# One ring of three PSUM banks for the scores and transposes of two attentions

## The chip, the cores and the metric

The kernel runs on one core of one Trainium2 chip. The metric is the device time of one execution in microseconds (us); a change is judged by the medians of repeated executions. Four engines matter here: TensorE (PE in the profile; PEld is its loading of stationary operands), VectorE (DVE), ScalarE (ACT), and the DMA queues that SyncE (SP), ScalarE and GpSimd (POOL) issue. Each engine works through its own queue of instructions in order and waits at an instruction until the semaphores that it names are there.

## The reference

One encoder block on 512 tokens of width 2048, in float32, batch 1. Cut to what matters here:

```python
h = rms_norm(x, norm1_w) * (1 + sc1) + sh1
qa, ka, va, qb, kb, vb, ga, gb = split(h @ w_in)          # 2048 -> 8704 columns
qa, ka = rope(rms_norm(qa, q_norm_w)), rope(rms_norm(ka, k_norm_w))
ya = softmax(qa @ ka.T / sqrt(128)) @ va                  # 8 heads, 2 key/value heads, all 512 keys
yb = softmax(qb @ kb.T / sqrt(128) + bias) @ vb           # 8 heads, a window of 8x16 keys per query
merged = sigmoid(ga) * (ya @ w_oa) + sigmoid(gb) * (yb @ w_ob)
x = x + g1 * (merged @ w_out)
x = x + g2 * swiglu(rms_norm(x, norm2_w) * (1 + sc2) + sh2)
out = rms_norm(x, final_w)
```

## The kernel before

**Products.** Every float32 operand of a matrix product is held as two tiles in the faster matmul format, a high part and the rest ("h" and "l" in the names: `h0h`, `h0l`). `split` (lines 165 to 170) makes them from a float32 source: ACT copies the high part (L168), DVE subtracts it from the source (L170). `mm3` (lines 184 to 190) then issues three matmuls, L188, L189 and L190, into one bank of PSUM. Weights come by DMA as `raw` tiles and are split into `whl` tiles on the way.

**Banks.** `bank(tag)` hands out the eight banks of PSUM: four named `mm`, two `S`, one `T`, one `Y`. Buffers of one name are handed out in turn, in the order in which the program asks for them, and the next holder of a bank waits until the last reader of the holder before is done.

**The stages around the change**, in the order of the program:

1. The projections of the first query heads, keys and part of the gates, up to about 299 us. `h0` to `h15` are the normalised activations, 128 features each.
2. Attention A, heads 0 to 3 (`att_a`, line 897). A head is four blocks of 128 queries. A block: the scores of 128 queries against 512 keys go into a bank `S` (L188 to L190, `S<-kh,qh`); `softmax` takes the maximum (DVE L862, negated at L863), the exponential with its sum (ACT L866), the reciprocal (DVE L869) and the scaled row (DVE L870, tile `e`); four transposes on PE (L886) put it into the bank `T`; `split` reads that bank into the tiles `pth` and `ptl`. The weighted sums of the values go into the bank `Y` (`Y<-pth,st`), 12 products of 256 columns for each two blocks, and `keep_y` stores them.
3. `gates(sg_a, GA, 12, 16)` (line 901): two passes over all of `h` for four column blocks of the first gate, in `mm` banks, each ending in two sigmoids (ACT L641, tile `go`). Then attention A, heads 4 to 7 (line 903), and the release of its memory, pool `p_a` (line 905).
4. `gates(sg_b, GB, 0, 4)` (line 954): two more such passes. While they run, the list `FORMS` (line 952) makes what the next stage needs, on DVE and ACT: `whole_features` adds high part and rest of `h` back into float32 (L928, tiles `hc` and `hw`), `feature_forms` makes sums and differences of their quarters (L938 to L941, tiles `sa` and `sb`) and splits them (`s05h`, `s07l` and so on, for the groups s = 0 to 3). These tiles lie in the pool `p_o` (line 924), in the memory that `p_a` leaves; a tile there waits for the last use of what it covers.
5. `gates7` and `values7` (lines 990 to 993): projections in a form with seven instead of eight block products (`group7`), by sums of weight blocks that `wforms` makes on DVE (tiles `ta`, `tb`, L696 to L699) and splits. For each group s the products go in the order `ORDER` = 1, 2, 3, 5, 6, 7, 4; product 3 needs `s07`, product 5 needs `s05` and the split of `ta`.
6. Attention B (`att_b`, line 1004), two heads at a time between the projections of the next two heads (lines 1085 to 1103). A half head: scores into a bank `S`, the bias added on the way out (DVE L1021), maximum, exponentials, scaling, four transposes into `T` (L1035), `split`, weighted sums in `Y`.
7. The output projections, the second norm, the SwiGLU and the last norm, from about 860 us.

**What sets the order.** The program is written stage after stage, but the framework lays out each engine's queue when it builds the program: an instruction may go ahead of others that were written earlier where the framework reckons these to be waiting for an operand or a bank. So products of the gate passes, which need nothing from the attentions, stand between the steps of the attentions on PE. This order is fixed before the run; on the chip an engine only waits.

Of the kernel before, what the change touches and what calls it, by code (L numbers as in the profile page):

```python
# [23 lines left out]
T = 512  # L24
# [88 lines left out]
def encoder_block(ctx: ExitStack, tc, xp, xT, c, ada1_w, ada2_w, b_ada, norm1_w, w_in, q_norm_w, k_norm_w, bias,  # L113
                  w_oa, w_ob, w_out, norm2_w, w_gate, w_up, w_down, final_w, rope, out):
    nc = tc.nc
    V, S, G = nc.vector, nc.scalar, nc.gpsimd
# [35 lines left out]
    def bank(tag):  # L152
        return ps.tile([P, 512], F32, tag=tag, name=tag, bufs={"mm": 4, "S": 2, "T": 1, "Y": 1}[tag])
# [12 lines left out]
    def split(hi, lo, src, eng=V, pin=lambda ins: ins):  # L166
        with tc.issue_after(hold[0].ins) if hold else contextlib.nullcontext():
            high = pin(S.activation(hi, src, AF.Copy))  # L168
        with tc.issue_after(hold[1].ins) if hold else contextlib.nullcontext():
            latest[:] = [high, pin(eng.tensor_sub(lo, src, hi))]  # L170

    def pair(pool, tag, width, bufs):
        return (pool.tile([P, width], F32R, tag=tag + "h", name=tag + "h", bufs=bufs),
                pool.tile([P, width], F32R, tag=tag + "l", name=tag + "l", bufs=bufs))
# [10 lines left out]
    def mm3(o, lh, ll, rh, rl, start, stop, n=0, **kw):  # L185
        if n:
            o, rh, rl = in_turn(o, n), streams(rh, n), streams(rl, n)
        nc.tensor.matmul(o, lh, rh, start=start, stop=False, **kw)  # L188
        nc.tensor.matmul(o, lh, rl, start=False, stop=False, **kw)  # L189
        nc.tensor.matmul(o, ll, rh, start=False, stop=stop, **kw)  # L190
# [24 lines left out]
    def slot():  # L215
        pace["due"] = min(pace["due"] + pace["rate"], 1.5)
        if mod["then"] and not fetched and mod["next"] == mod["end"]:
            mod.update(mod["then"].pop())
        if pace["due"] >= 1 and (fetched or mod["next"] < mod["end"]):
            pace["due"] -= 1  # L220
            advance(mods)
# [140 lines left out]
    def fetch():  # L362
        while len(fetched) < mod["loads"] and mod["next"] < mod["end"]:
            n = mod["next"] + {2: 32, 3: 32, 4: -32, 5: -32}.get(mod["next"] // KT, 0)
            w = mod["mw"].tile([P, 1024], F32, tag="mw", name="mw", bufs=mod["loads"])
            mod["queue"].dma_start(w, ada2_w[n * P:(n + 1) * P, :])  # L366
            fetched.append(w)
            mod["next"] += 1
# [485 lines left out]
    def keep_y(h, yb):  # L854
        o = aside.tile([P, T], F32, tag="y", name="yo")
        S.activation(o.rearrange("p (h e i) -> p h e i", e=2, i=P), apart(yb), AF.Copy)
        nc.scalar.dma_start(y_d[h], o)

    def softmax(pool, src, scale, w, bufs=2):

        mx = small.tile([P, 1], F32, tag="mx", name="mx")
        V.reduce_max(mx, src, axis=AX.X)  # L862
        V.tensor_scalar(mx, mx, -scale, None, op0=ALU.mult)  # L863
        e = pool.tile([P, 512], F32, tag="e", name="e", bufs=bufs)[:, :w]
        sm = small.tile([P, 1], F32, tag="sm", name="sm")
        S.activation(e.rearrange("p (e i) -> p e i", e=2), src.rearrange("p (i e) -> p e i", e=2), AF.Exp, bias=mx, scale=scale,  # L866
                     accum_out=sm)
        rs = small.tile([P, 1], F32, tag="rs", name="rs")
        V.reciprocal(rs, sm)  # L869
        V.tensor_scalar(e, e, rs, None, op0=ALU.mult)  # L870
        return e

    def att_a(h, q, j, kv):
        kh, kl = (t[:, kv * T:(kv + 1) * T] for t in kT)
        vs = slice(kv * HD, (kv + 1) * HD)
        pts = []
        for i in range(NT):
            if i % 2 == 0:
                pts.append(pair(p_a, "pt", 2 * T, 3))
            sl = slice(j * T + i * P, j * T + (i + 1) * P)  # L880
            sc = bank("S")
            mm3(sc, q[0][:, sl], q[1][:, sl], kh, kl, True, True, T)
            e = softmax(p_a, sc, SCALE, T)
            tp = bank("T")
            for k in range(NT):
                nc.tensor.transpose(tp[:, k * P:(k + 1) * P], e[:, k * P:(k + 1) * P], ident)  # L886
            hi, lo = (t.rearrange("p (k q) -> p k q", k=NT)[:, :, i % 2 * P:(i % 2 + 1) * P] for t in pts[-1])
            split(hi, lo, tp.rearrange("p (k q) -> p k q", k=NT))
        yb = bank("Y")
        for n, pt in enumerate(pts):  # L890
            ys = yb[:, n * 256:(n + 1) * 256]
            for k in range(NT):
                ks = slice(k * 256, (k + 1) * 256)
                mm3(ys, vA[k][0][:, vs], vA[k][1][:, vs], pt[0][:, ks], pt[1][:, ks], k == 0, k == NT - 1, 256)
        keep_y(h, yb)

    for h in range(4):
        att_a(h, q, h, 0)
# [4 lines left out]
    for h in range(4):  # L903
        att_a(4 + h, q, h, 1)
# [95 lines left out]
    mod.update(mw=p_w, sums=[(p_w, 1), (p_w0, 1)], end=48, loads=3)  # L1000
    fetch()
    p_b = tc.alloc_tile_pool(name="p_b", bufs=1, side="right")

    def att_b(h, q, k, v, vs):

        bm = p_b.tile([P, 512], F32, tag="bm", name="bm", bufs=2)
        nc.scalar.dma_start(bm, bias[h * P:(h + 1) * P, :])
        edge = bm.rearrange("p (g n) -> p g n", g=2)
        inner = edge[:, 1:2].to_broadcast([P, 2, 256])
        by = lambda t: t.rearrange("p (k n) -> p k n", n=P)  # L1010
        rows_of = lambda t, g: t[:, g * P:(g + 1) * P]
        keys_of = lambda t, g: by(t)[:, g - 1:g + 1] if g else by(t)[:, 0::3]
        pt = pair(p_b, "pt", 1024, 2)
        for gs, b2, o in (((1, 2), inner, 512), ((0, 3), edge, 0)):
            sc = bank("S")
            for n, g in enumerate(gs):
                mm3(sc[:, n * 256:(n + 1) * 256].rearrange("p (i e) -> p i e", e=2), *(rows_of(t, g) for t in q),
                    *(keys_of(t, g).rearrange("p e i -> p i e") for t in k), True, True)
            s = p_b.tile([P, 512], F32, tag="sb", name="sb", bufs=2)
            s2v = s.rearrange("p (g n) -> p g n", g=2)  # L1020
            V.scalar_tensor_tensor(s2v, sc.rearrange("p (g n) -> p g n", g=2), SCALE, b2, op0=ALU.mult, op1=ALU.add)  # L1021
            mx, sm, rs = (small.tile([P, 2], F32, tag=t, name=t) for t in ("mx2", "sm2", "rs2"))
            V.reduce_max(mx, s2v, axis=AX.X)
            V.tensor_scalar(mx, mx, -1.0, None, op0=ALU.mult)
            e = p_b.tile([P, 512], F32, tag="e", name="e", bufs=3)
            for n in range(2):
                S.activation(e[:, n * 256:(n + 1) * 256].rearrange("p (e i) -> p e i", e=2),
                             s[:, n * 256:(n + 1) * 256].rearrange("p (i e) -> p e i", e=2), AF.Exp, bias=mx[:, n:n + 1],
                             accum_out=sm[:, n:n + 1])
            V.reciprocal(rs, sm)  # L1030
            for n in range(2):
                V.tensor_scalar(e[:, n * 256:(n + 1) * 256], e[:, n * 256:(n + 1) * 256], rs[:, n:n + 1], None, op0=ALU.mult)
            tp = bank("T")
            for j, at in enumerate((0, 1, 2, 3) if o else (2, 3, 1, 0)):
                nc.tensor.transpose(tp[:, j * P:(j + 1) * P], e[:, at * P:(at + 1) * P], ident)  # L1035
            split(*(t[:, o:o + 512] for t in pt), tp)
            slot()
        yb = bank("Y")
        for n, (kk, at, to) in enumerate(((1, slice(5, 7), slice(2, 4)), (0, slice(3, 5), slice(1, 3)),
                                          (2, slice(0, 8, 7), slice(0, 4, 3)), (3, slice(1, 3), slice(0, 2)))):  # L1040
            mm3(by(yb)[:, to], v[kk][0][:, vs], v[kk][1][:, vs], *(by(t)[:, at] for t in pt), n == 0, n == NT - 1,
                skip_group_check=True)
        o = aside.tile([P, T], F32, tag="y", name="yo")
        for to, src in ((o[:, :320], yb[:, 192:]), (o[:, 320:], yb[:, :192])):
            S.activation(to, src, AF.Copy)
        nc.scalar.dma_start(y_d[8 + h], o)
# [628 lines left out]
```

## Time and profile before

| | us |
|---|---|
| median of 3 runs | 2465.59 (2464.08 to 2469.82) |
| the profiled execution, its own time | 2474.1 |
| its span, first to last instruction | 2472.3 |
| PE busy in the span | 2435.4 |
| DVE busy | 2007.5 |
| ACT busy | 1069.9 |

The profiled execution took 8.5 us (0.34%) more than the median, and 1.8 us of it lie outside its span. Sums below are made against its rows; the difference that they give is then put on the median. Two things help to read it. A matmul's end is modelled, and matmuls overlap: a product of 512 columns is shown 0.38 us long, and the next one starts 0.22 us after it, so PE can lose some tenths of a microsecond between two products and still be shown busy. And every view gives times from the start of the span, so a stage is read by its stretch.

### The profile page before, as it was taken

The page shows a single profiled execution, that of the slowest core. Times are in us where ns is not written, and L with a number is a line of the kernel's source. Part 1 is how long each engine was busy: PE and PEld are TensorE (multiplying, and loading weights), DVE is VectorE, ACT ScalarE, POOL GpSimd, SP SyncE. Part 2 cuts the span into 40 slices and gives each one's busy share as a digit, 9 for nine tenths or more (in the row PEclk, how much of TensorE's full clock was granted, in tenths as well). Part 3 has the DMA queues.
Part 4 walks back from the last instruction along what each step waited for, and adds up shares of the span by engine and source line. Part 5 has one row for each costly group of instructions (what it writes and reads, how often), then busy time and mean ns, then how long its engine had stood idle before and what let it go on. Part 6 is the DMA issues. An engine that isn't in the chain of part 4 may idle for free.

```text
span 2472.3 us, 42367 instructions
## 1 busy us (share of the span) xinstructions
PE 2435.4 (99%) x17327; PEld 2280.1 (92%) x17327; DVE 2007.5 (81%) x2704; ACT 1069.9 (43%) x1466; POOL 150.9 (6%) x255
## 2 busy tenths in 40 slices
PE   7999999999999999999999999999999999999998
PEld 6888888999888888888999999999999998999997
DVE  7995778999677678667899989889989885687877
ACT  5223455544344523237744444444444454433333
POOL 0100000000011111111000000000000010000010
PEclk9999999999999999999999999999999999999999
DMA  9874322455766687867444444445454466546563
GB/s 357 285 253 144 104 89 80 142 185 181 252 211 231 204 302 248 296 215 228 137 154 155 145 162 147 135 147 163 129 171 147 128 196 214 188 155 233 189 250 121
DMA packets 213730, 461.77 MB, mean 187 GB/s; under 512 B 15152, under 2 KB 59552, under 8 KB 204832
## 3 DMA queue, kind: packets, MB, share of 16 engines
q1 hardware_dynamic: 174160, 309.76, 38.4%
q0 software_dynamic: 29872, 132.73, 15.8%
q10 hardware_dynamic: 9504, 16.58, 1.9%
q8 instruction: 136, 2.23, 0.4%
q14 instruction: 58, 0.48, 0.1%
HBM read 412.84 MB, written 46.17 MB: 186 GB/s over the span
## 4 chain that ended last, share of the span: by engine, by line
PE 72%; DVE 14%; issue 6%; DMA 4%; ACT 1%; POOL 0%; DVEq 0%; POOLq 0%; ACTq 0%
PE mm L190 15%; PE mm L189 15%; PE mm L188 15%; PE S L188 6%; PE S L189 6%; PE S L190 6%; DVE whl L170 4%; PE Y L188 3%; PE Y L189 2%; PE Y L190 2%; DVE raw L524 2%; DMA raw<-in_w_down 2%; DMA raw<-in_w_up 1%; PE T L886 1%; DVE g_acc L631 1%
## 5 line engine op out<-in xcount | busy, mean ns | idle before, releaser
L168 ACT ACTIVATE whl<-raw 128x1024 fp32r<-128x1024 f32 (+1 forms) x483 | 453.9, 943 | 671.1 <-PE mm L190 288.4
L170 DVE TENSOR_TENSOR whl<-raw,whl 128x1024 fp32r<-128x1024 f32 (+1 forms) x483 | 517.9, 1087 | 126.3 <-ACT whl L168 125.9
L168 ACT ACTIVATE whl<-ta 128x1024 fp32r<-128x1024 f32 x124 | 131.4, 1059 | 181.8 <-PE mm L190 107.6
L168 ACT ACTIVATE whl<-tb 128x1024 fp32r<-128x1024 f32 x124 | 131.4, 1060 | 174.5 <-PE S L190 109.8
L170 DVE TENSOR_TENSOR whl<-ta,whl 128x1024 fp32r<-128x1024 f32 x124 | 151.2, 1220 | 40.7 <-ACT whl L168 40.1
L388 DVE SCALAR_TENSOR_TENSOR acc<-mw,cact,acc 128x1024 f32<-128x1024 f32 x124 | 158.8, 1281 | 18.3 <-DMA mw<-in_ada_w 17.9
L170 DVE TENSOR_TENSOR whl<-tb,whl 128x1024 fp32r<-128x1024 f32 x124 | 150.9, 1217 | 4.6 <-ACT whl L168 4.5
L366 POOL DMA_DIRECT2D mw<-in_ada_w x113 | 60.3, 534 | 1361.5 <-DVE acc L388 946.5
L697 DVE TENSOR_TENSOR ta<-raw,ta 128x512 f32<-128x512 f32 x124 | 85.2, 687 | 69.3 <-DMA raw<-in_w_down 29.7
L696 DVE TENSOR_TENSOR ta<-raw 128x512 f32<-128x512 f32 x124 | 85.3, 688 | 36.7 <-DMA raw<-in_w_down 34.3
L188 PE MATMUL mm<-x56h,whl 128*128 128x256 f32 x336 | 92.5, 275 | 0.4 <-DVE c L784 0.4
L189 PE MATMUL mm<-x56l,whl 128*128 128x256 f32 x336 | 92.4, 275 | 0.0
L190 PE MATMUL mm<-x56h,whl 128*128 128x256 f32 x336 | 92.4, 275 | 0.0
L189 PE MATMUL mm<-whl,s 128*128 128x256 f32 x320 | 88.2, 276 | 1.0 <-DVE whl L170 0.8
L188 PE MATMUL mm<-x3h,whl 128*128 128x256 f32 x320 | 88.1, 275 | 0.0
L188 PE MATMUL mm<-whl,s 128*128 128x256 f32 x320 | 88.1, 275 | 0.0
L189 PE MATMUL mm<-x3l,whl 128*128 128x256 f32 x320 | 88.0, 275 | 0.0
L190 PE MATMUL mm<-x3h,whl 128*128 128x256 f32 x320 | 88.0, 275 | 0.0
L188 PE MATMUL S<-x56h,whl 128*128 128x256 f32 x320 | 88.0, 275 | 0.0
L189 PE MATMUL S<-x56l,whl 128*128 128x256 f32 x320 | 88.0, 275 | 0.0
L190 PE MATMUL S<-x56h,whl 128*128 128x256 f32 x320 | 88.0, 275 | 0.0
L190 PE MATMUL mm<-whl,s 128*128 128x256 f32 x320 | 88.0, 275 | 0.0
(1879 smaller groups left out, 8910.9 us busy)
## 6 DMA issues: line engine op xcount, KB each, us to landing
raw<-in_w_in SPq DMA_DIRECT2D x133, 512.0 KB, 4.6
mw<-in_ada_w POOLq DMA_DIRECT2D x113, 512.0 KB, 4.5
raw<-in_w_gate SPq DMA_DIRECT2D x92, 512.0 KB, 4.6
raw<-in_w_up SPq DMA_DIRECT2D x88, 512.0 KB, 4.6
raw<-in_w_down SPq DMA_DIRECT2D x88, 512.0 KB, 5.4
raw<-in_ada_w POOLq DMA_DIRECT2D x29, 1024.0 KB, 6.6
raw<-in_w_out SPq DMA_DIRECT2D x48, 512.0 KB, 5.5
ffd<-c SPq DMA_DIRECT2D x10, 1024.0 KB, 4.8
```

The lines of the kernel that those rows point to most:

```text
L168: high = pin(S.activation(hi, src, AF.Copy))
L170: latest[:] = [high, pin(eng.tensor_sub(lo, src, hi))]
L188: nc.tensor.matmul(o, lh, rh, start=start, stop=False, **kw)
L189: nc.tensor.matmul(o, lh, rl, start=False, stop=False, **kw)
L190: nc.tensor.matmul(o, ll, rh, start=False, stop=stop, **kw)
L366: mod["queue"].dma_start(w, ada2_w[n * P:(n + 1) * P, :])
L388: behind(V.scalar_tensor_tensor(acc, part, cact[:, k:k + 1], acc, op0=ALU.mult, op1=ALU.add))
L524: V.scalar_tensor_tensor(raw, raw, 1.0, call, op0=ALU.mult, op1=ALU.mult, accum_out=y)
L631: V.tensor_add(acc, acc, b)
L696: V.tensor_sub(t1, b12, b11)
L697: V.tensor_sub(t2_, b22, t1)
L886: nc.tensor.transpose(tp[:, k * P:(k + 1) * P], e[:, k * P:(k + 1) * P], ident)
```

## The change

The scores and the transposes of both attentions ask for their banks by `bank(next(turns))`, where `turns` goes round S, S, T, in place of `bank("S")` for all scores and `bank("T")` for all transposes. Since two asks for `S` take the two `S` banks in turn, this is one ring of three banks, in the order in which the program asks: scores of block 0, transposes of block 0, scores of block 1, transposes of block 1, and so on.

```diff
+    turns = itertools.cycle("SST")
+
     def att_a(h, q, j, kv):
...
-            sc = bank("S")
+            sc = bank(next(turns))
             mm3(sc, q[0][:, sl], q[1][:, sl], kh, kl, True, True, T)
             e = softmax(p_a, sc, SCALE, T)
-            tp = bank("T")
+            tp = bank(next(turns))
...
     p_b = tc.alloc_tile_pool(name="p_b", bufs=1, side="right")
+    turns = itertools.cycle("SST")
...
-            sc = bank("S")
+            sc = bank(next(turns))
...
-            tp = bank("T")
+            tp = bank(next(turns))
```

No operation is added or taken away by hand, and no other bank, tile or loop is touched. Scores of block i + 2 now take the bank that the transposes of block i had, so they wait until these are split; before, they took the bank of the scores of block i, and waited for its exponential alone. Transposes of a block wait for the exponential of the block before, and no longer for the split of that block's transposes.

The diff does not show what the framework makes of it. The queues of PE, DVE and ACT are laid out anew from the first block of attention A to `gates7`, and again through attention B. Three places follow. The lines of the changed file are two higher in this part (`L928` is `L930`, `L886` is `L888`).

On PE, the end of attention A: the last weighted sums of head 7 (`Y_3685`), and what stands behind them. `mm_3715` and `mm_3716` are the first pass of `gates(sg_b)`, `mm_3852` and `mm_3853` the second and last one; `mm_4041` is the first product of `gates7`. Before:

```order
L188 MATMUL Y_3685<-pth_3643,st_2434 128x256
L189 MATMUL Y_3685<-ptl_3644,st_2434 128x256
L190 MATMUL Y_3685<-pth_3643,st_2434 128x256
L188 MATMUL mm_3716<-h12h_1507,whl_3814 128x512
L189 MATMUL mm_3716<-h12l_1508,whl_3814 128x512
L190 MATMUL mm_3716<-h12h_1507,whl_3814 128x512
```

And with the change:

```order
L190 MATMUL Y_3685<-pth_3643,st_2434 128x256
L190 MATMUL mm_3853<-h14h_1698,whl_3976 128x512
L188 MATMUL mm_3852<-h15h_1713,whl_3976 128x512
L189 MATMUL mm_3852<-h15l_1714,whl_3976 128x512
L190 MATMUL mm_3852<-h15h_1713,whl_3976 128x512
L188 MATMUL mm_3853<-h15h_1713,whl_3976 128x512
L189 MATMUL mm_3853<-h15l_1714,whl_3976 128x512
L190 MATMUL mm_3853<-h15h_1713,whl_3976 128x512
L188 MATMUL mm_4041<-h0h_372,whl_4058 128x256
```

Before, 117 products of 512 columns stand between the last weighted sum and the first product of `gates7`: the end of the first pass, from `h12`, and the whole second pass. With the change 7 are left; the other 110 stand further ahead, between the blocks of heads 0 to 7.

On DVE, in the forms: the splits of the first and second group. Before:

```order
L170 TENSOR_TENSOR s05l<-sa,s05h 128x1024
L170 TENSOR_TENSOR s07l<-sb,s07h 128x1024
L928 TENSOR_TENSOR hc<-h11h,h11l 128x512
L170 TENSOR_TENSOR whl<-raw,whl 128x1024
L938 TENSOR_TENSOR sa<-hw 128x512
L940 TENSOR_TENSOR sb<-hw 128x512
L939 TENSOR_TENSOR sa<-sa,hw 128x512
L170 TENSOR_TENSOR whl<-raw,whl 128x1024
L941 TENSOR_TENSOR sb<-hw,sa 128x512
L170 TENSOR_TENSOR s15l<-sa,s15h 128x1024
L170 TENSOR_TENSOR whl<-raw,whl 128x512
L170 TENSOR_TENSOR s17l<-sb,s17h 128x1024
```

And with the change:

```order
L170 TENSOR_TENSOR s05l<-sa,s05h 128x1024
L170 TENSOR_TENSOR s07l<-sb,s07h 128x1024
L930 TENSOR_TENSOR hc<-h9h,h9l 128x512
L930 TENSOR_TENSOR hc<-h10h,h10l 128x512
L930 TENSOR_TENSOR hc<-h11h,h11l 128x512
L940 TENSOR_TENSOR sa<-hw 128x512
L942 TENSOR_TENSOR sb<-hw 128x512
L941 TENSOR_TENSOR sa<-sa,hw 128x512
L943 TENSOR_TENSOR sb<-hw,sa 128x512
L170 TENSOR_TENSOR s15l<-sa,s15h 128x1024
L170 TENSOR_TENSOR s17l<-sb,s17h 128x1024
```

The splits of gate weights (`whl`) that stood between the forms are gone from here, four in all between the first `hc` and the split of the first `ta`; they stand ahead of the end of attention A now. In both queues all forms stand behind the last split of attention A.

On ACT, the sigmoids of the first gate pass (`go`). Before, they stand behind the last block of head 3:

```order
L856 ACTIVATE yo<-Y 128x512
L168 ACTIVATE qh<-T 128x4x128
L857 DMA y_2440<-yo 128x512
L641 ACT_TABLE_LOAD
L641 ACTIVATE go<-mm 128x512
L168 ACTIVATE qh<-T 128x4x128
```

With the change the first one stands in head 1:

```order
L866 ACTIVATE e,sm<-T,mx 128x512
L641 ACT_TABLE_LOAD
L641 ACTIVATE go<-mm 128x512
L168 ACTIVATE pth<-S 128x4x128
L866 ACT_TABLE_LOAD
L866 ACTIVATE e,sm<-S,mx 128x512
L642 DMA sga_264<-go 128x512
```

A sigmoid between two exponentials brings a table load ahead of it and one behind it. The whole ACT queue has 13 table loads before and 19 with the change; the six more stand in attention A.

## Prediction

> **What bounds the kernel now.** I read the page first, then a table of stretches, then the waits in the two attentions, then the chain that ended last, and then single instructions where that chain leaves PE. The page's span, busy times and shares of the chain:
>
> ```profile
> span 2472.3 us, 42367 instructions
> ...
> PE 2435.4 (99%) x17327; PEld 2280.1 (92%) x17327; DVE 2007.5 (81%) x2704; ACT 1069.9 (43%) x1466; POOL 150.9 (6%) x255
> ...
> PE 72%; DVE 14%; issue 6%; DMA 4%; ACT 1%; POOL 0%; DVEq 0%; POOLq 0%; ACTq 0%
> ```
>
> PE is the bound nearly everywhere, with little to win: 2472.3 less 2435.4 is 37 us for the whole program. The table of stretches (busy time with count for each engine, then granted clock, DMA share, GB/s) has attention A, the rest of the gate passes, the beginning of `gates7`, attention B, and a stretch that I need for the clock:
>
> ```profile
> core 0: us, PE busy (x) PEld busy (x) DVE busy (x) ACT busy (x) POOL busy (x), PEclk, DMA share, GB/s
> 290.00:416.30 126.30, 125.16 (x715) 103.52 (x714) 93.29 (x220) 76.45 (x170) 0.53 (x1) 1.00 0.23 76
> 416.30:441.60 25.30, 25.30 (x120) 22.16 (x119) 25.20 (x35) 13.26 (x15) 0.00 (x0) 1.00 0.34 106
> 441.60:447.10 5.50, 4.43 (x40) 4.24 (x38) 5.50 (x9) 3.60 (x6) 0.00 (x0) 1.00 0.55 148
> 660.00:860.00 200.00, 198.60 (x1017) 168.68 (x1016) 144.50 (x222) 94.00 (x184) 25.26 (x44) 1.00 0.66 218
> 50.00:53.40 3.40, 3.40 (x9) 2.65 (x9) 3.40 (x5) 0.47 (x1) 0.53 (x1) 0.50 0.79 259
> ```
>
> In attention A PE stands idle 126.30 − 125.16 = 1.1 us, in attention B 1.4 us. The stretch 416.3 to 441.6, behind attention A, is the odd one: DVE is busy 25.20 of 25.30 us there, and all of the next 5.5, in which PE idles 1.07. The chain of waits says the same: at 416.57 it goes over to DVE and walks along the forms.
>
> ```profile
> 416.57 2.44 DVE hc L928 x4
> ...
> 441.10 1.13 DVE s27l L170
> ```
>
> So from the end of attention A to the first groups of `gates7` DVE sets the end, and PE only fits because it has the gate passes to do meanwhile. PE's rows at both ends of that stretch (start, length, idle time before):
>
> ```profile
> 416.19 0.28 PE L190 MATMUL Y<-pth,st 128*128 128x256 f32 x1
> 416.31 0.38 PE L188 MATMUL mm<-h12h,whl 128*128 128x512 f32 x1
> ...
> 441.56 0.27 PE L188 MATMUL mm<-h0h,whl 128*128 128x256 f32 x1
> ...
> 445.69 0.28 PE L189 MATMUL mm<-s05l,whl 128*128 128x256 f32 x1
> 447.04 0.38 PE L190 MATMUL mm<-s05h,whl 128*128 128x256 f32 x1 [1.07 <-DVE whl L170]
> ```
>
> The last weighted sum starts at 416.19. 117 gate products run from 416.31 to 441.56, 0.216 us each. The 38 products of `gates7` that can run before the split of `ta` take 441.56 to about 445.80. Then PE waits for that split until 447.04: the cover was 1.2 us too short.
>
> **The tail of attention A.** The change moves 110 of the 117 products ahead of that last weighted sum; 7 remain. The forms can't follow them forward. On DVE they stand behind the last split of attention A, and the first one starts only when the weighted sum that began at 416.19 (0.28 long) is through. DVE's rows, from the first form on, and the row of ACT that the split of `s15` waits for:
>
> ```profile
> 416.51 0.69 DVE L928 TENSOR_TENSOR hc<-h0h,h0l 128x512 f32<-128x512 f32 x1
> ...
> 428.66 1.22 DVE L170 TENSOR_TENSOR whl<-raw,whl 128x1024 fp32r<-128x1024 f32 x1
> 429.80 0.68 DVE L938 TENSOR_TENSOR sa<-hw 128x512 f32<-128x512 f32 x1
> ...
> 431.00 0.68 DVE L939 TENSOR_TENSOR sa<-sa,hw 128x512 f32<-128x512 f32 x1
> 431.61 1.22 DVE L170 TENSOR_TENSOR whl<-raw,whl 128x1024 fp32r<-128x1024 f32 x1
> 432.74 0.68 DVE L941 TENSOR_TENSOR sb<-hw,sa 128x512 f32<-128x512 f32 x1
> ...
> 434.48 0.68 DVE L170 TENSOR_TENSOR whl<-raw,whl 128x512 fp32r<-128x512 f32 x1
> 435.08 1.21 DVE L170 TENSOR_TENSOR s17l<-sb,s17h 128x1024 fp32r<-128x1024 f32 x1
> ...
> 438.75 1.22 DVE L170 TENSOR_TENSOR whl<-raw,whl 128x1024 fp32r<-128x1024 f32 x1
> 439.88 1.22 DVE L170 TENSOR_TENSOR s25l<-sa,s25h 128x1024 fp32r<-128x1024 f32 x1
> ```
> ```profile
> 431.72 1.06 ACT L168 ACTIVATE s15h<-sa 128x1024 fp32r<-128x1024 f32 x1 [4.44 <-DVE sa L939]
> ```
>
> From the first form (416.51) to the product that waits for the `ta` split (447.04) DVE takes 30.53 us. Four splits of gate weights leave this stretch; from start to next start they take 1.14 + 1.13 + 0.60 + 1.13 = 4.0 us. One wait comes in: with the `whl` split gone, `s15l` follows `sb` at once, 1.2 us after the start of `sa` at 431.00, while ACT's half of it ends at 432.78, 1.8 us after: 0.6 us. So DVE needs 30.53 − 4.0 + 0.6 = 27.1 us, and it starts 0.32 us after the last weighted sum (416.51 − 416.19).
>
> PE has 7 × 0.216 = 1.5 us of gate products and the 4.24 us of `gates7` (445.80 − 441.56), from 0.12 us after that sum. It is ready for the `ta` split at 5.9 us and gets it at 27.4 us. The wait is 21.5 us where it was 1.2: **+20.3 us.** The same from the other side: the attention ends 110 × 0.216 = 23.7 us later, and DVE's chain behind it is 3.4 shorter. The wait falls into two: some 5 us at the first `s07` product (ACT's `s07h` is ready about 9 us after the sum, PE 4.3 after it) and about 15 at `s05`. The removed splits cost nothing where they now stand: DVE is idle 126.30 − 93.29 = 33 us in attention A and gains 23.7 us of room there.
>
> **The clock after the gap.** One more row of PE, ahead of the stretch at 50.0 that the table shows at clock 0.50:
>
> ```profile
> 49.08 0.48 PE L600 MATMUL mm<-whl,h2h 128*128 128x512 f32 x1 [3.35 <-ACT whl L168]
> ```
>
> After 3.35 us without work PE ran 3.4 us at half its clock, which loses 1.7 us. Gaps of 5 and 15 us should bring this at least once where PE has work: **+1.7 us**, bounds 0 (it falls into the wait) and 3.4 (twice).
>
> **Attention A itself.** The waits in 290 to 416.3, first of PE, then of its loading of stationary operands, which a running product covers in part:
>
> ```profile
> PE S L188 <- ACT e L866: 0.4, 1, 0.4
> ```
> ```profile
> PEld T L886 <- DVE ptl L170: 5.1, 17, 0.4
> PEld S L188 <- ACT e L866: 2.6, 8, 0.8
> ```
>
> The wait of transposes for the split of those before (17 times) is what a second bank takes away; visible on PE is only 0.4 us of all this. I count −1, and at most −8 (5.1 + 2.6). Against it stands the chain from scores to transposes of one block:
>
> ```profile
> 374.65 0.38 PE L190 MATMUL S<-kh,ql 128*128 128x512 f32 x1
> 375.07 0.69 DVE L862 TENSOR_REDUCE mx<-S 128x1 f32<-128x512 f32 x1 [0.55 <-PE S L190]
> ...
> 376.31 0.69 ACT L866 ACTIVATE e<-S,mx 128x512 f32<-128x512 f32 x1 [0.21 <-DVE mx L863]
> ...
> 377.53 0.48 DVE L870 TENSOR_SCALAR e<-e,rs 128x512 f32<-128x512 f32 x1
> ```
>
> Without other work between: 0.42 to the maximum, 0.69 for it, some 0.2 for the negation, 1.22 from exponential to scaling, 0.48: 3.0 us. Where the scores lie in `T`, the new order of PE often puts 11 weighted sums (0.11 each) and 6 gate products between them and their transposes, 2.7 us with the last score product itself. About ten of 32 blocks are so tight: 10 × 0.3 = +3 us. Then the table loads:
>
> ```profile
> 371.58 1.28 ACT L866 ACT_TABLE_LOAD   x1 [0.18 <-DVE mx L863]
> 372.88 0.69 ACT L866 ACTIVATE e<-S,mx 128x512 f32<-128x512 f32 x1
> ```
>
> Six more at 1.28 us are 7.7 us of ACT, which is busy 76 of 126 us here. They come at three places where two or more microseconds of gate products stand on PE anyway; I count +0.5 at each, +1.5 in all, and 7.7 at most. The Trainium skill's page "ScalarE: Activation LUTs", section "What ACT_TABLE_LOAD costs", has a drain of about 1.38 us beside the load at every switch; by it the most would be 16 us, and the sum about 2 us higher. The trace shows no such drain: the exponential starts at 372.88, right behind the load, so the row decides.
>
> Attention A: −1 + 3 + 1.5 = **+3.5 us**. Bounds: −8, and 32 × 0.3 + 7.7 = +17.
>
> **Attention B.** Its order has gate or projection products enough on every side, and its end isn't followed by work that hangs on it: the next products are of `w_oa`. PE's waits there for the attention come to this row:
>
> ```profile
> PE T L1035 <- ACT e L1027: 0.8, 2, 0.4
> ```
>
> I take **0**, between −1 (its 0.8 gone) and +5 (16 half heads at 0.3). The rest of the program keeps its order.
>
> Sum: 20.3 + 1.7 + 3.5 + 0 = +25.5 us on the profiled 2474.1. That execution lies 8.5 us over the median; the difference goes on the median: 2465.6 + 25.5 = **2491.1 us**, 1% slower.
>
> **The rivals.** First, the ring pays in the attentions. The Trainium skill's page "Perfetto Trace Analysis", section "Optimizing Tensor Performance", says that independent groups of matmuls should rotate through different banks, so that the evacuation of one overlaps the next. It speaks for this change. As a mechanism here: the 7.7 us of waits above and 0.8 in attention B go, and the tight blocks don't show. Then 20.3 + 1.7 − 8.5 = +13.5 us, 2479 us. For it: 17 of 32 transposes do wait for a split. Against it: PE's own row shows hardly any of that. 5%.
>
> Second, it costs more in the attentions: every block waits and the table loads stand on the path, to the upper bounds of A and B. 20.3 + 3.4 + 17 + 5 = +46 us, 2511 us; I take all above +37 for this. For it: the chain of a block is now in one line with the split of the one two before. Against it: there are 23.7 us more of gate products in the stretch. 9%.
>
> Third, not slower: the forms aren't held by the last weighted sum. If the pool's tiles lay only over tiles that are read early, and DVE came to the forms under the last heads, the stretch of 27.1 us would be covered again, as before. The point from which it decides is a first `hc` 20 us or more ahead of the last `Y` product; then −1 to −8 of the attentions stay, 2458 to 2465 us. Against it: the row of 416.51 starts as that product ends (416.19 + 0.28), and the queue has all forms behind the last split. 3%, two of which would show as faster.
>
> Last, that nothing moves: the rows of the order under the change say otherwise. 1%, 2465.6 us.
>
> **The numbers.** The forecast (+15.4 to +36.4: the tail at 20 to 21.5, the clock 0 to 3.4, the attentions from −5 to +12, not all ends at once) has 82%, more than that 9%, less but still slower 5%, no change or faster 4%. The range 2481 to 2502 us leaves out about 18%. A measurement of this kernel can tell about 0.2%, 5 us, from no change: faster 2%, the same 2%, slower 96%.
>
> **What would show it.** Right: a first `hc` just behind the last `Y` product of head 7; DVE unbroken from there for 27 us; PE idle about 5 us at the first `s07` product and about 15 at the first L190 of `s05`, released by `whl` L170; then a stretch of clock 0.50; attention A later in ending by about 24 us, with PE's idle time in it by a few microseconds over 1.1; attention B as before. Wrong: PE idle under 10 us between attention A and the second group of `gates7`, or a difference that sits in the attentions or behind 860 us.

## The result and the profile after

The changed kernel takes 2499.24 us (median of 4 runs, 2497.56 to 2502.53) against 2466.61 us before (4 runs, 2464.08 to 2469.82): 1.0133 times as long, 95% interval 1.0116 to 1.0151, or 32.6 us more. The profiled execution took 2499.32 us, 25 us more than the profiled one before. The page, in the three lines that the prediction showed of before:

```profile
span 2497.5 us, 42404 instructions
...
PE 2440.6 (98%) x17327; PEld 2281.6 (91%) x17327; DVE 2015.6 (81%) x2704; ACT 1081.0 (43%) x1472; POOL 151.0 (6%) x255
...
PE 70%; DVE 15%; issue 7%; DMA 3%; ACT 2%; POOL 0%; DVEq 0%; ACTq 0%; POOLq 0%
```

PE's busy time has grown by 5 us, the span by 25: PE waits. The table of stretches (start and end, length, busy time and count of PE, PEld, DVE, ACT and POOL, granted clock, DMA share, GB/s) says where. Its rows are attention A, two parts of the gap behind it, the first products after the gap, and attention B:

```profile
288.00:440.70 152.70, 149.02 (x813) 120.92 (x812) 101.74 (x222) 88.32 (x176) 0.53 (x1) 1.00 0.23 73
440.70:450.00 9.30, 4.66 (x34) 4.13 (x32) 9.06 (x14) 4.97 (x6) 0.00 (x0) 1.00 0.50 172
450.00:468.20 18.20, 4.09 (x18) 3.64 (x17) 17.70 (x25) 6.45 (x8) 0.00 (x0) 0.50 0.09 27
468.20:474.00 5.80, 5.80 (x43) 5.80 (x43) 5.80 (x9) 2.10 (x3) 0.00 (x0) 0.80 0.35 99
694.00:874.30 180.30, 177.07 (x913) 149.86 (x913) 131.63 (x205) 81.61 (x162) 23.02 (x40) 1.00 0.61 197
```

Attention A holds 110 instructions of PE more and is 29 us longer; in the 27.5 us behind it PE has 8.75 us of work, and DVE hardly a pause. PE's waits between 440.7 and 475 us (what it waited for: us in total, times, longest):

```profile
PE mm L188 <- ACT whl L168: 12.8, 1, 12.8
PE mm L188 <- ACT s07h L168: 4.6, 1, 4.6
PE mm L189 <- DVE s07l L170: 1.3, 1, 1.3
```

The chain of waits walks along the forms, as the prediction drew it, and ends at the product that waited 12.8 us:

```profile
440.72 0.13 PE Y L190
440.87 2.49 DVE hc L930 x4
443.36 2.41 DVE hw L930 x4
...
462.78 1.14 DVE s27l L170
...
465.76 1.06 ACT whl L168
466.87 0.58 PE mm L188
```

For the comparison of all kernels I use one more figure: the time between the starts of consecutive PE instructions of a stretch, less what the same instructions take when packed (0.2155 us for 512 columns, 0.1115 for 256, 0.109 for 128, the medians of neighbours in these traces). What is left is time that PE lost there. "Attention A" runs from its first score to its last weighted sum, "the tail" from there to about the first L190 of `s05`, the product that waits for the split of `ta`, and "groups behind" over the products with forms that follow. Us lost, and in the first column the length of attention A and the time of one row of it (128 queries of one head, 32 rows; the mean of the 31 steps from scores to scores):

```
kernel                         A, a row     to A's norm  A     tail   groups behind  B     the rest
before                         123.5, 3.69   21.5         8.3   1.4    0.8           8.0    13.9
before, a second execution     123.6, 3.69   17.6         8.3   1.4    0.8           7.9    11.2
after                          152.5, 4.67   16.9        13.6  21.4    1.4          10.7    15.4
ring in A alone                152.5, 4.67   17.3        13.6  21.4    2.3           8.0     7.3
ring in B alone                123.5, 3.69   18.9         8.3   1.4    0.8          10.7    10.8
ring, gate pass held back      151.4, 4.65   17.5        31.7   3.6    1.9          10.7    11.2
ring, later forms later        152.5, 4.67   18.1        13.5   6.4   14.8          10.9    11.7
skewed ring in A               123.8, 3.77   16.3         8.6   1.4    0.8           8.0     8.6
ring, no scaling in A          139.5, 4.21   16.9         9.7  13.3    1.2          10.7    10.7
before, no scaling in A        123.0, 3.67   19.8         7.8   1.4    0.8           8.1     6.5
skewed ring in B               123.5, 3.69   17.2         8.3   1.4    0.8           9.4     8.2
skewed ring in both            123.8, 3.77   17.1         8.6   1.4    0.8           9.4     6.1
ring, no sigmoid in gates      144.1, 4.43   18.1        12.1  15.4    1.2          10.7    12.0
```

So the change costs 5.3 us in attention A, 20.0 in its tail, 0.6 in the groups behind and 2.7 in attention B: 28.6 us. The two outer columns differ by up to 5 and 9 us among kernels that are alike there; the profiled execution before had the largest loss of all at the start, and so the two profiled executions stand 25 us apart, the medians 32.6. In two kernels, those with the gate pass held back and without the sigmoid, some 1.4 us more are lost where no column counts, between the norm and attention A; the clock stands at half there for 3.4 us.

The mean of a row hides one long step: between heads 3 and 4 stand most products of the first gate (`sg_a`), 34.2 us in the kernel before and 18.6 us in the changed one, which has more of them between the rows ahead. The other 30 steps take 2.67 us each before and 4.21 after.

### The profile page after: what moved, and what is told of

Same layout as the page of the kernel before. It is cut to its first block, busy times and chain, and to the rows that moved or that the text cites. A ratio compares the mean times of both kernels' runs of the same rounds, so it can differ in the third digit from the quotient of the medians.

```text
span 2497.5 us, 42404 instructions
## 1 busy us (share of the span) xinstructions
PE 2440.6 (98%) x17327; PEld 2281.6 (91%) x17327; DVE 2015.6 (81%) x2704; ACT 1081.0 (43%) x1472; POOL 151.0 (6%) x255
## 4 chain that ended last, share of the span: by engine, by line
PE 70%; DVE 15%; issue 7%; DMA 3%; ACT 2%; POOL 0%; DVEq 0%; ACTq 0%; POOLq 0%
PE mm L190 14%; PE mm L188 14%; PE mm L189 14%; PE S L189 5%; PE S L190 5%; PE S L188 5%; DVE whl L170 3%; PE Y L188 2%; PE Y L189 2%; PE Y L190 2%; DVE raw L524 2%; DMA raw<-in_w_down 2%; DMA raw<-in_w_up 1%; PE T L188 1%; PE T L190 1%
## 5 line engine op out<-in xcount | busy, mean ns | idle before, releaser
L168 ACT ACTIVATE whl<-raw 128x1024 fp32r<-128x1024 f32 (+1 forms) x483 | 454.1, 943 | 664.1 <-PE mm L190 281.0
L188 PE MATMUL mm<-x56h,whl 128*128 128x256 f32 x336 | 92.6, 276 | 0.4 <-DVE c L784 0.4
L190 PE MATMUL mm<-x56h,whl 128*128 128x256 f32 x336 | 92.4, 275 | 0.0
L188 PE MATMUL mm<-x3h,whl 128*128 128x256 f32 x320 | 88.1, 275 | 0.3 <-DVE c L782 0.3
L188 PE MATMUL mm<-whl,s 128*128 128x256 f32 x320 | 88.1, 275 | 0.0
L190 PE MATMUL mm<-x3h,whl 128*128 128x256 f32 x320 | 88.0, 275 | 0.0
L188 PE MATMUL S<-x56h,whl 128*128 128x256 f32 x320 | 88.0, 275 | 0.0
L190 PE MATMUL S<-x56h,whl 128*128 128x256 f32 x320 | 88.0, 275 | 0.0
L190 PE MATMUL mm<-whl,s 128*128 128x256 f32 x320 | 88.0, 275 | 0.0
```

## The experiments

Each ratio below is to executions of the kernel before that were taken beside the kernel in question. Their medians lie between 2465.5 and 2467.9 us, so a ratio need not be the quotient of two medians given here, and a difference from the changed kernel's 2499.24 us carries 1 to 2 us of that.

**Theory T1**, the prediction's: 110 gate products, moved ahead of the last weighted sum, leave DVE's forms uncovered. **Rival R1**: the ring costs in both attentions alike. **Rival R2** grew from the prediction's own second rival: the ring itself slows the rows of attention A, and the gate products only fill the holes. First, one part of the change alone.

**The ring in attention A alone.** Attention B goes back to fixed banks:

```diff
-            sc = bank(next(turns))
+            sc = bank("S")
...
-            tp = bank(next(turns))
+            tp = bank("T")
```

> The ring stands in attention A alone; attention B keeps two banks for scores and one for transposes. Theory T1 (the gate products that the ring moves ahead of the last weighted sum leave the forms of the features uncovered: +20.0 us in the tail, and +5.3 us of waits in attention A): 2466.6 + 25 to 27 = 2492 to 2494 us, with the wait of 21 us ahead of the first form products as in the changed kernel. Rival R1 (the ring costs in both attentions alike, and the tail is only where it shows): half of the 32.6 us, about 2483 us.

2490.98 us, 1.0092 times before (1.0059 to 1.0126), with the same loss in attention A and in the tail as the whole change, to 0.1 us. That is 1 us under the range of T1 and 8 us over R1's number: R1 falls.

**The ring in attention B alone**: the same edit in attention A, attention B with the ring.

> The ring stands in attention B alone; attention A and the gate products behind it are as before. T1: no forms of features lie behind attention B, so only its own waits grow, by the 2.7 us that the two traces differ by in that stretch and up to 2 us behind it: 2469 to 2472 us, and no wait of more than 2 us ahead of the first form products. R1: about half of the 32.6 us, 2483 us. If neither: 2466.6 within 0.2%, so that the 2.7 us belonged to attention A's later end.

2470.24 us, 1.0008 times before (0.9988 to 1.0029). The interval holds no change, so the time alone doesn't show a loss (the medians stand 3.4 us apart); the trace does, 10.7 us against 8.0 in that stretch and no other difference in the fixed columns. PE waits there for the scaling ahead of the transposes; these are rows of the changed kernel's waits in attention B:

```profile
PE T L1038 <- DVE e L1035: 1.1, 3, 0.4
...
PE S L1038 <- DVE e L1035: 0.6, 2, 0.4
```

**The gate pass held back.** If only the order of the gate products did the harm, putting them back should undo it. Here the second gate pass is laid out behind the last weighted sum, which the kernel keeps in `last_y` (the lines that keep it are not shown):

```diff
-    gates(sg_b, GB, 0, 4)
+    gates(sg_b, GB, 0, 2)
+    with tc.issue_after(last_y[0].ins):
+        gates(sg_b, GB, 2, 4)
```

> The changed kernel, with the second pass of the gate product (96 products and the 24 rows around them) queued behind the last weighted sum of attention A, as 141 rows were before the change; 120 rows are now there instead of 31. T1 in its simple form (only the cover is lost, the ring's own chain costs 5.3 us): 89 products x 0.2155 us = 19.2 us of the 21.5 us wait ahead of the first form products go, the attention keeps its time apart from the products that left it, 2499.2 - 19 = 2480 us. Rival R2 (the ring's chain from scores to transposes is too long for attention A, and the gate products were drawn in to fill its waits): the products' places stay empty, waits of scores and transposes of 15 to 20 us appear in attention A, and the time stays at 2495 to 2500 us.

2496.93 us, 1.0116 times before (1.0081 to 1.0150): R2's number, and not distinct from the changed kernel's. The stretches of this kernel, attention A and what lies behind it up to the product that waits for the first group's weights:

```profile
290.20:441.60 151.40, 135.85 (x721) 109.06 (x720) 99.45 (x220) 85.24 (x173) 0.53 (x1) 0.95 0.22 71
441.60:470.60 29.00, 26.62 (x140) 23.39 (x139) 29.00 (x41) 14.69 (x17) 0.00 (x0) 0.97 0.22 67
```

The same two stretches of the changed kernel:

```profile
288.10:440.60 152.50, 148.82 (x812) 120.72 (x810) 101.74 (x222) 88.22 (x176) 0.53 (x1) 1.00 0.23 73
440.60:468.20 27.60, 8.85 (x52) 7.86 (x50) 26.76 (x38) 11.42 (x14) 0.00 (x0) 0.67 0.23 77
```

About 90 instructions have gone from the first stretch to the second, and the tail is filled again (26.62 of 29.00 us). But attention A is hardly shorter: 151.40 against 152.50 us. The edit reaches its last eight rows: the 24 ahead of them take 114.1 us in both kernels, with the same products but for two. The last eight take 37.3 us here, without a gate product among them; 38.4 us in the changed kernel, with 87, which are 18.7 us of PE; and 27.7 us in the kernel before, with 38. PE now waits where the products were (waits of PE, then of its loading):

```profile
PE S L890 <- DVE e L870: 6.7, 9, 2.7
PE T L890 <- DVE rs L869: 2.3, 1, 2.3
PE T L890 <- DVE e L870: 2.1, 2, 1.7
```
```profile
PEld S L890 <- ACT e L866: 5.0, 3, 3.0
```

17.8 us are gained in the tail and 18.1 lost in the attention. The granted clock of 0.95 can be a part of the second: it stands at half for 13.6 us of the last eight rows, which is 6.8 us at the most, and without that these rows would still be longer than before. The simple form of T1 is wrong: the products are not what makes the ring's rows long, for without them the rows keep nearly all their length.

**Why a row takes longer (T2).** The ring gives banks in the order in which they are asked for: scores 0, transposes 0, scores 1, transposes 1, scores 2. With three banks the scores of row i+2 get the bank of the transposes of row i, and wait until these are split. Before, they took the bank of scores i, free after the exponential. The changed kernel's trace, the split on DVE, and the next scores in the same bank `T`, first the loading of their stationary operand and then the product:

```profile
395.14 0.69 DVE L170 TENSOR_TENSOR ptl<-T,pth 128x512 fp32r<-128x512 f32 x1 [0.65 <-ACT pth L168]
```
```profile
395.88 0.19 PEld L188 LDWEIGHTS T<-kh,qh 128*128 128x128 f32 x1 [0.30 <-DVE ptl L170]
395.88 0.48 PE L188 MATMUL T<-kh,qh 128*128 128x512 f32 x1
```

The split ends at 395.83, the scores start at 395.88, and what their loading waited for is that split. In the kernel before, scores start at 393.15. The split of the row three before starts at 393.96, that of the row two before at 397.41, both behind them:

```profile
393.15 0.38 PE L188 MATMUL S<-kh,qh 128*128 128x512 f32 x1
```
```profile
393.96 0.68 DVE L170 TENSOR_TENSOR ptl<-T,pth 128x512 fp32r<-128x512 f32 x1
...
397.41 0.69 DVE L170 TENSOR_TENSOR ptl<-T,pth 128x512 fp32r<-128x512 f32 x1 [1.09 <-ACT pth L168]
```

Over all rows: in the changed kernel none of 30 scores starts before the split of the row two before has ended, and 13 start within 0.2 us of it (the others later); before, 28 of 30 start ahead of that end, by 4.5 us in the median of all. The queue that the framework lays out shows the same: PE has the scores of the next row ahead of the transposes of this one in 30 of 31 places before, and in 13 with the ring. From the start of its scores to the end of its split a row takes 6.6 us in the changed kernel (median), 9.75 before; with a row each 4.67 and each 3.69 us that is (by the means) 1.5 rows under way against 2.7. The ring makes a row's own way shorter and yet the attention longer, for it keeps fewer rows under way.

**The skewed ring.** T2 says that not the shared banks but the order of asking does it. So, in attention A, the scores of row i+1 ask for their bank ahead of the transposes of row i (shown against the changed kernel; the tiles `pt` of a head are also asked for ahead of the loop, which is not shown):

```diff
+        def turn_round(i, e):
             tp = bank(next(turns))
...
             sc = bank(next(turns))
             mm3(sc, q[0][:, sl], q[1][:, sl], kh, kl, True, True, T)
-            e = softmax(p_a, sc, SCALE, T)
+            if waiting:
+                turn_round(*waiting.pop())
+            waiting.append((i, softmax(p_a, sc, SCALE, T)))
+        turn_round(*waiting.pop())
```

> A ring of three in attention A, asked for in another order: the scores of row i+1 before the transposes of row i (attention B keeps two banks and one). Scores i+3 then take the bank of the transposes of row i, and no longer scores i+2. Theory T2 (what costs is that scores i+2 wait for the split of row i, so that two rows are under way instead of three and a row takes 4.67 us instead of 3.69 us): with three rows under way attention A is back at 3.7 to 3.8 us a row, 141 rows of gate products and others stand behind its last weighted sum, the wait ahead of the form products is 1 to 2 us, and the time is that before, 2466.6 within 5 us. Rival R4 (a shared ring costs whatever its order, since every bank is held by both kinds of step and each PE wait meets the slower one): a row stays above 4.4 us and the time is 2485 to 2495 us, as with the ring in attention A alone.

2464.47 us, 1.0006 times before (0.9996 to 1.0016): the whole loss is gone, with the same three banks. Its two stretches, and after them those of before:

```profile
287.50:411.30 123.80, 122.48 (x701) 101.15 (x700) 94.57 (x218) 75.00 (x163) 0.53 (x1) 1.00 0.23 73
411.30:442.50 31.20, 30.13 (x161) 26.80 (x160) 31.10 (x44) 17.39 (x20) 0.00 (x0) 1.00 0.39 118
```
```profile
292.70:416.20 123.50, 122.36 (x702) 101.06 (x701) 92.48 (x218) 74.37 (x164) 0.53 (x1) 1.00 0.22 73
416.20:447.40 31.20, 30.13 (x161) 26.80 (x160) 31.10 (x43) 17.16 (x20) 0.00 (x0) 1.00 0.39 117
```

They are one picture: a row takes 3.77 us, 25 of 30 scores start ahead of the split of the row two before, PE has the next scores ahead of the transposes in 29 of 31 places, and the gate products stand behind the last weighted sum again without being held there. T2's count was too high, though: 2.0 rows are under way on average, not three, and that is enough here.

**A shorter chain, with the ring and without.** If a row takes what its chain takes divided by the rows under way, a shorter chain must pay with the ring and not before:

```diff
-        rs = small.tile([P, 1], F32, tag="rs", name="rs")
-        V.reciprocal(rs, sm)
-        V.tensor_scalar(e, e, rs, None, op0=ALU.mult)
         return e
```

> The changed kernel without the reciprocal and the scaling of the exponentials in attention A (its weights are left undivided). The chain from scores to split is shorter by 0.15 + 0.49 us and the two hand-overs, about 0.7 us. T2 (two rows under way: a row takes half the chain): 0.35 us less a row, x 32 rows = 11 us less, 2488 us, and fewer gate products ahead of the last weighted sum. R1 or R3 (something other than the chain, in the tail alone): the chain's length does not matter, 2498 to 2500 us.

> The kernel before, without the same two steps in attention A (its weights are left undivided). T2: with three rows under way attention A is bound by TensorE's own work, so a shorter chain gives nothing: 2466.6, not more than 3 us less. If VectorE's share or the chain's length bound it there too: 5 us less or more.

With the ring 2485.4 us, 13.8 less (1.0085 times before, 1.0071 to 1.0098, where the change has 1.0133), and in the trace 12.0 us less in attention A and its tail: a row takes 4.21 us, 0.46 less. Before 2468.76 us, 1.0015 times (1.0006 to 1.0024): no gain; its trace has 0.5 us less in attention A. Of the 12.0 us 3.9 lie in attention A and 8.1 in its tail. The sizes are near those expected, and the contrast is T2's.

**The table loads.** The prediction counted six more of them at 1.5 us in all:

```diff
-            S.activation(o, b, AF.Sigmoid)
+            S.activation(o, b, AF.Copy)
```

> The changed kernel with a plain copy in place of the sigmoid of the gate products that attentions A and the products ahead of them hold (their gates stay without the sigmoid), so that ScalarE need not load another table and then the exponential's again: 12 table loads of 1.28 us stand in attention A, against 6 before the change. The prediction put the six more loads at 1.5 us. T2: a load that meets a row's chain delays two rows under way by half of 1.28 us; nine loads gone at most, 0 to 6 us less: 2493 to 2499 us. If the loads were the main price of the ring: the full 11.5 us or more, 2488 us or less.

2491.32 us, 7.9 less (1.0096 times before, 1.0081 to 1.0110); the trace has 7.5 us less in attention A and its tail. ScalarE's groups of table loads around attention A, in the changed kernel and here:

```profile
L866 ACT ACT_TABLE_LOAD x6 | 7.7, 1283 | 2.8 <-DVE mx L863 2.7
L641 ACT ACT_TABLE_LOAD x5 | 6.4, 1283 | 0.5 <-ACT yo L856 0.4
```
```profile
L866 ACT ACT_TABLE_LOAD x2 | 2.6, 1283 | 0.0
```

Nine loads fewer, eight of them in attention A, are worth 0.83 us each, more than half their 1.28 us: the result lies between what T2 and its rival gave. Of the 7.5 us only 1.5 lie in attention A; 6.0 lie in the tail, where 39 gate products stand and no longer 7. At 0.83 us six loads are an estimated 5 us. The loads are a part of the ring's price, but not most of it.

**The tail's other cure.** In the gap the first group's weights stand on DVE behind forms that later groups need. Here these come one group at a time (the second group's features also take the tile of the first, which is not shown):

```diff
-    FORMS = [None, None, wf(0), wf(1), ff(0), wf(2), ff(1), ff(2), wf(3), ff(3)]
+    both = lambda n: lambda: (whole_features(n), feature_forms(n))
+    FORMS = [None, None, both(0), None, None, None, None, None, both(1), both(2), both(3)]
```

> The changed kernel, with the forms of the second to fourth group of features made after the first group's products are queued and no longer ahead of the first group's weights; the second group uses the first one's tile. T1: the first form product of the second half waits for VectorE's queue, in which 21 instructions of later groups (451.2 to 463.8 us, 12.6 us) stand ahead of the weights' forms; without them the wait falls from 21.5 us to about 9 us, 2499.2 - 12.6 = 2486.6 us, unless the later groups are late in their turn (each has 18 us of products ahead of it). Rival R3 (the weights' DMA or the clock sets the first product's time, and VectorE's queue only fills the wait): 2497 to 2500 us.

2495.05 us, 1.0104 times before (1.0070 to 1.0137): 4.2 us less, a third of what T1 gave and too little to tell from the changed kernel, whose 1.0133 lies in the interval. In the trace the gap itself shrinks by 15.0 us, more than the 12.6 expected, but the groups behind it lose 13.4 us more. This kernel's waits of PE from 440 to 700 us:

```profile
PE mm L188 <- ACT whl L168: 5.4, 4, 2.1
PE mm L188 <- ACT s07h L168: 2.4, 1, 2.4
PE mm L189 <- DVE s17l L170: 1.4, 1, 1.4
PE mm L189 <- DVE s27l L170: 1.4, 1, 1.4
```

Each later group is now late in its turn, as the expectation allowed: DVE is busy 72.2 of the 75.9 us from 454.1 to 530 us, and moving its work only spreads the wait.

**The kernel before, executed again**, without an edit:

> The kernel before once more, for a second trace. If the first stretch of the profiled execution before (21.5 us beyond the packed pitch up to the first transposes of the rotary step, against 16.9 to 18.9 us in the changed kernels) was one execution's own, this one lies at 17 to 19 us there; if the ring's kernels were in fact faster there, at 21 us again. Attention A, the tail and attention B agree with the first trace within 0.1 us.

17.6 us at the start, so the 21.5 was the first execution's own; attention A, tail and attention B agree within 0.1 us.

**The skewed ring in B, alone and with A.** Within a head of attention B the second scores ask ahead of the first transposes; the second kernel has this and the skewed ring in A:

```diff
             sc = bank(next(turns))
...
+            if waiting:
+                turn_round(*waiting.pop())
...
-            tp = bank(next(turns))
...
-            slot()
+            waiting.append((o, e))
+        turn_round(*waiting.pop())
```

> The ring in attention B alone, with the second scores of a head asked for before the first transposes (attention A keeps two banks and one). T2: the 2.7 us that the plain ring costs in attention B's stretch go, for three steps are under way again: 2466 us within 2 us, the stretch at 8.0 us or less beyond the packed pitch. Rival R4 (any shared ring costs there): 10.7 us beyond the packed pitch, as with the plain ring.

> The skewed ring in both attentions. T2: the sum of the two parts, 2464 to 2467 us: no gain over two banks and one, since TensorE is at its packed pitch in attention A either way (8.3 us beyond it before, 8.6 us with the skewed ring). If the third bank for scores were worth something: 3 us less than before or more.

In B alone 2467.08 us, 0.9998 times before (0.9988 to 1.0007); in both 2467.8 us, 1.0003 times (0.9993 to 1.0014). The trace has 9.4 us in attention B, between the two values expected: half of the plain ring's loss stays there, and no run shows why. No ring tried here beats two banks and one.

## Why the prediction was right, and where it was not

**The total** was forecast at +25.5 us with +15.4 to +36.4 around it; the fixed stretches give +28.6, the medians +32.6. The direction and most of the size came from one step, the tail. The other terms missed by a few microseconds, and not all to the same side: the groups behind, with the clock, +0.6 where 1.7 was forecast, attention A +5.3 for 3.5, attention B +2.7 for 0.

**The tail: right.** +20.3 was forecast, +20.0 measured. The forms start at 440.87, right behind the last weighted sum, and the first L190 of `s05`, which needs the split of `ta`, at 468.13: 27.3 us later (27.1 forecast). The waits are 4.6 and 1.3 us at `s07` (some 5) and 12.8 at `s05` (some 15). The long one stands one step earlier than forecast, at the first L188 of `s05`, which waits for ACT's half of that split. The rest is the clock.

**The clock: inside the tail, not on top of it.** 18 products, 12 of `s07` and the first six behind the wait, took 4.09 us at half clock, where the packed pitch gives 2.0, but DVE set the end there anyway: its split of `ta` runs from 466.85 for 1.23 us, and the L190 follows at 468.13. Behind the gap 43 products took 5.80 us against 4.8 packed: +1.0 of the forecast 1.7.

**Attention A: the mechanism was in the rivals, and its price was put too low.** The forecast had +3.5 us, the trace +5.3. The gain of 1 us from the transposes' waits doesn't show: the skewed ring, which has the second bank for transposes too, loses 8.6 us there against 8.3 before. Without it the prediction's other two terms come to 4.5. The six table loads were put at 1.5 us, and by the run without them an estimated 1.0 us of theirs lies in attention A; another 4 us lie in the tail, where the prediction didn't count them.

**The step that failed is the cause.** The prediction took the move of 110 products for what the change does, and the uncovered forms for its price. But held back, the products left the attention's last eight rows nearly as long as with them, 37.3 against 38.4 us, where they take 27.7 before. What the ring does is to slow the rows, and the move fills them: attention A is 29 us longer, 23.7 of it is gate products, and these are then missed behind it. The prediction had this chain in its second rival ("in one line with the split of the one two before"), but asked only whether it would bring more waits on top, and set the 23.7 us of gate products against it as cover. They were cover, once: used in the attention, they were gone from the tail. The sum came out right all the same, since the order of the products was known beforehand and the tail follows from where they stand, whatever moved them there.

**Attention B: too low.** 0 was forecast, between −1 and +5; the trace has +2.7, in the ring's runs with B each time.

**The first rival** had the ring pay. The Trainium skill's page "Perfetto Trace Analysis", section "Optimizing Tensor Performance", would have independent groups of matmuls rotate through banks. The plain ring does so and is slower; the skewed one does so too and is the same. The row that decides is 122.36 busy of 123.50 us: PE waited 1.1 us there before, and little was left to win.

What stays open is the difference of 4 us between the fixed stretches' 28.6 and the medians' 32.6. It lies within what the start and the rest of the program vary by, and within the interval (28.6 to 37.2 us), and no run isolates it.

## What to carry to other kernels

Banks taken in turn are given in the order of asking, so count which step's release each request waits for: a ring of three asked for as scores, transposes, scores, transposes makes the scores wait for the split of the row two before, and asked for one row ahead for that of the row three before. Here that was 1.5 against 2.0 rows under way, and the whole loss. Measure the time of one row of the pipeline, not only the idle time of the bound engine, since filler work from behind the stage hides a slower row in it and is then missing where it came from. A product order that looks like the cause may be a symptom: hold it back once and see whether the stage gets shorter.

## What the runs showed of the hardware

The half clock lasted far longer than the one the prediction went by. In the records of the granted clock of the changed kernel it stands at 0.50 for 20.5 us in one piece, from about 450 to 470.5 us, across the 12.8 us wait; the stretch after 50.0 in the kernel before had 3.4 us. With the ring in attention A alone, whose tail is the same, it is 23.9 us. The Trainium skill's page "TensorE: Matmul & The Clock Gate", section "Terms", puts the penalty at about the throttled time by the part of the clock that is missing, an estimate of 10 us here. The trace shows about 3 us on products, 2 of them in a stretch that DVE ended: PE had little to run at that clock.

Attention A's length came out at 123.5, 123.5, 123.5 and 123.6 us in four traces with two banks and one, and its tail at 31.2 us in each; the start of the program and its rest differed between the same executions by 4 and 6 us. A difference of a few microseconds is found in the stretch, not in the total.
